# A hybrid decoder layer on one core: keeping split weights in DRAM, and a triangular inverse spread over 128 partitions

## The chip, the cores and the metric

The kernel runs on one core of one Trainium2 chip. The metric is the device time of one execution in microseconds, taken as the median of several runs.

## The reference

One decoder layer works on 2,048 tokens of width 1,024, in float32. It has two mixers side by side and a feed-forward part behind them:

```python
h = _rmsnorm(x, norm1_w[l])
proj = h @ w_in[l]                      # 1024 x 3840 columns, for HGRN2 and RWKV-7
q_raw, f_raw, i_raw, g_raw = ...        # HGRN2: 4 heads of 128, chunkwise gated recurrence
o_hg = _hgrn2_mixer(...)                # S_t = diag(f_t) S_{t-1} + k_t v_t^T ; o_t = S_t^T q_t
rw_p = rw_p + (_token_shift(rw_p) - rw_p) * rw_shift_mu[l]
o_rw = _rwkv7_mixer(...)                # S_t = S_{t-1} diag(w_t) + (S_{t-1} a_t) b_t^T + v_t k_t^T
x = x + concat([o_hg, o_rw]) @ w_out[l]
x = x + _conv_ffn(_rmsnorm(x, norm2_w[l]), w_up[l], conv_w[l], conv_b[l], w_down[l])
return _rmsnorm(x, final_norm_w)
```

RWKV-7 has 8 heads of 64. Its recurrence is solved chunk by chunk; for each chunk of 64 tokens a unit triangular matrix is inverted.

## The kernel before

The tokens are cut into four blocks of 512. The first part, `phase1`, does the input projection, both mixers and three of the four output projections; the second part does the last output projection, the FFN and the closing norm. Only `phase1` is edited.

Every large matmul is made of three. A float32 operand is split into a high part `h` (a cast on ScalarE, line 243) and a low part `l` (a subtraction on VectorE, line 244), and `mm3` adds h·h, h·l and l·h (lines 259 to 261).

Three generators run side by side in `phase1`, and a loop takes one step of each of two of them in turn and then fills about 2 us with the third:

- `dense` is the stream of projections. Each block has 30 columns of 128 output features. For a column, `load` (line 546) brings the weights from `w_in` in two halves of 256 KB into `wraw`, a ring of four buffers, and splits each into `wh` and `wl`, rings of four buffers each; so two columns fit, and the raw ring runs ahead of them. A column is 24 large matmuls. The same 30 columns come again in every block, and are loaded and split again. Between the columns stand the output projections of earlier blocks (`out_block`, which loads `woraw`), transposes and norms.
- `rw_super` is RWKV-7, two super-blocks a block, eight in all. It makes the matrices `M` (matmuls of line 695), sends a part of them by DMA through DRAM (`Ed`, lines 711 and 713) into `E`, where 64 partitions hold one 32 x 32 triangle each (two of the four 32 x 32 quarters per chunk are triangles), and inverts them on VectorE in 31 steps of a product (line 764) and a sum (line 766) into `Ti`. Then `Ti` and its transpose `TiT` go to DRAM (`Td`, lines 770 and 772) and come back in another layout, into `TZ` (line 782, 4 transfers) and `TTs` (line 779, 8 transfers). Matmuls `z` (line 790), `z2` (line 803) and `qu` (line 816) put the inverse together and apply it; ScalarE copies the result out of PSUM into `M` and `UV`; `yg` (line 841) and a scan of eight steps (line 875) follow.
- `hg_unit` is HGRN2, four heads a block. Six levels of doubling (`scaled`, lines 934 to 939) scale q and k by products of the gates; each level is four VectorE products of half a block's elements: X for odd and even positions, `Sf` and `Pf`.

All weight loads and nearly all other transfers go through the queue of the sync engine (SP), which issues them in order and stops at the first whose buffer or source is not ready. GpSimd is nearly without work in the kernel before. The order of each engine's instructions is set by a scheduler from the program's order and the dependencies.

Of the kernel before, what the change touches and what calls it, by code (L numbers as in the profile page):

```python
# [18 lines left out]
P = 128  # L19
# [4 lines left out]
NBLK = T // BLK  # L24
# [37 lines left out]
def tile_layer(ctx, tc, consts, x, norm1_w, w_in, hg_lb_logits, hg_norm_w, rw_shift_mu, rw_w0, rw_w2,  # L62
# [46 lines left out]
    def act(out_, in_, func, **kw):  # L109

        want = tables.get(func)
        if want is not None and want != tab["now"]:
            pre = S.preload_act_table_set(want)
            for u_ in tab["uses"]:
                tc.add_manual_dep(pre.ins, u_.ins.name, NOSYNC, reason="table order")
            tab.update(now=want, pre=pre, uses=[])
        i_ = S.activation(out_, in_, func, **kw)
# [121 lines left out]
    def split(pool, src, shape, name, bufs):  # L239

        hi = pool.tile(shape, F32R, tag=name + "h", name=name + "h", bufs=bufs)
        lo = pool.tile(shape, F32R, tag=name + "l", name=name + "l", bufs=bufs)
        S.copy(hi, src)  # L243
        V.tensor_sub(lo, src, hi.bitcast(F32))  # L244
        return hi, lo
# [17 lines left out]
    def phase1(c1):  # L263
        hp = c1.enter_context(tc.tile_pool(name="hp", bufs=1, reuse_waits="tile"))
        wp = c1.enter_context(tc.tile_pool(name="wp", bufs=2, reuse_waits="tile"))
        sp = c1.enter_context(tc.tile_pool(name="sp", bufs=1, reuse_waits="tile"))
        rp = c1.enter_context(tc.tile_pool(name="rp", bufs=1, reuse_waits="tile"))
# [10 lines left out]
        TTs = hp.tile([P, 16, 64], F32, name="TTs")  # L278
# [4 lines left out]
        hl = hp.tile([P, KD, BLK], F32R, name="hl")  # L283
# [214 lines left out]
        def dense():  # L498
# [37 lines left out]
            for i, jb in sorted(extra, key=lambda e: e[0], reverse=True):  # L536
                jobs.insert(i, jb)
            cols = [jb[1] for jb in jobs if jb[0] == "P"]
            loaded = {}

            def load(i):
                if i < len(cols) and i not in loaded:
                    ws = []
                    for k2 in range(2):
                        raw = wp.tile([P, 4, P], F32, tag="wraw", name="wraw", bufs=4)
                        dma(raw, w_in[0, k2 * 512:k2 * 512 + 512, cols[i]:cols[i] + P].rearrange("(k p) c -> p k c", p=P))
                        ws.append(split(wp, raw, [P, 4, P], "w", 4))
                    loaded[i] = ws

            i = 0  # L550
            load(0)
            ahead = iter(())
            for n, jb in enumerate(jobs):
# [26 lines left out]
                ws = loaded.pop(i)  # L580
# [24 lines left out]
        er0 = lambda e: 64 if e == 0 else 0  # L605
# [5 lines left out]
        def col0(u, e):  # L611

            return er0(e) if u == 0 else 64 - er0(e)
# [3 lines left out]
        U = range(2)  # L617

        def rw_super(nb, s_):

            tl = stage[("tl", nb)]
            r, k, v = (stage.pop(("rkv", nb, s_, w)) for w in range(3))
# [10 lines left out]
            a, iW = ai[:, 0], ai[:, 1]  # L633
# [9 lines left out]
            c, km, sq = mk_[:, 0], mk_[:, 1], mk_[:, 2]  # L643
# [70 lines left out]

            KBT = tile_("KBT", [2, 8, P], "KBT")
            for u in U:
# [7 lines left out]
            UV = tile_("UV", [8, 2, P], "UV")  # L724
# [18 lines left out]
            for b, h, e, u in quads():  # L743
                kr, c0, sl = 64 - er0(e), col0(u, e), (b * 2 + h) * 64
# [5 lines left out]
            for e in range(2):  # L750
                r0, c0 = er0(e), col0(1, e)
                act(RHS[r0:r0 + 64, 4:8, :, 64:128], lvv[c0:c0 + 64, 1], AF.Copy)
            yield

            n = 64
            Ti = rp.tile([P, 32, 32], F32, tag="Ti", name="Ti")
            V.memset(Ti[0:n], 0.0)
            V.memset(Ti[0:n].rearrange("m a b -> m (a b)")[:, 0:1024:33], 1.0)
            yield
            for j in range(31):  # L760
                nr, ncol = 31 - j, j + 1
                tmp = rp.tile([P, 272], F32, tag="etmp", name="etmp")
                tv = tmp[0:n, 0:nr * ncol].rearrange("m (a b) -> m a b", b=ncol)
                V.tensor_mul(tv, E[0:n, j, j + 1:32].unsqueeze(2).broadcast_to([n, nr, ncol]),
                             Ti[0:n, j, 0:ncol].unsqueeze(1).broadcast_to([n, nr, ncol]))
# [4 lines left out]
            dma(Td[0], Ti[0:n])  # L770
            V.tensor_copy(TiT[0:n], Ti[0:n].rearrange("m a b -> m b a"))
            dma(Td[1], TiT[0:n])
            TZ = tile_("XH", [2, 2, 4, 2, 32], "TZ")
            for u in U:
                for e in range(2):
                    r0 = er0(e)
                    for q in range(2):
                        m0 = u * 32 + (e * 2 + q) * 8
                        dma(TTs[r0 + 32 * q:r0 + 32 * q + 32, 8 * u:8 * u + 8, 32 * q:32 * q + 32],
                            Td[1, m0:m0 + 8].rearrange("m s t -> s m t"))  # L780
                    m0 = u * 32 + e * 16
                    dma(TZ[r0:r0 + 32, 0, u].rearrange("p b h t -> p (b h) t"),
                        Td[0, m0:m0 + 8].rearrange("m s t -> s m t"))
            for _ in range(2):
                yield
            z = bank2()
            for b, h, e, u in quads():
                r0 = er0(e)
                c0, sl = r0 + 32 - 32 * u, u * 256 + (b * 2 + h) * 32
                TE.matmul(z[c0:c0 + 32, 0, sl:sl + 32], M[r0:r0 + 32, u, e, b, h, 32:64],  # L790
                          TZ[r0:r0 + 32, 0, u, b, h, :], start=True, stop=True, tile_position=(r0, c0))
            for u in U:
                for e in range(2):
                    r1 = er0(e) + 32
                    c0 = r1 - 32 * u
                    act(TZ[r1:r1 + 32, 1, u].rearrange("p b h t -> p (b h t)"),
                        z[c0:c0 + 32, 0, u * 256:u * 256 + 256], AF.Copy)
            yield
            z2 = bank2()
            for b, h, e, u in quads():  # L800
                r0 = er0(e)
# [4 lines left out]
            for u in U:  # L806
                for e in range(2):
                    r0 = er0(e)
# [5 lines left out]
            for b, h, e, u in quads():  # L814
                r0, c0, sl = er0(e), col0(u, e), ((b % 2) * 2 + h) * P
                TE.matmul(qus[u][c0:c0 + 64, b // 2, sl:sl + P], TTs[r0:r0 + 64, u * 8 + b * 2 + h, :],
                          RHS[r0:r0 + 64, 4 * u + b, h, :], start=True, stop=True, tile_position=(r0, c0))
            for u in U:
                quv = qus[u].rearrange("p j (b h t) -> p (j b) h t", h=2, t=P)
                bs = slice(4 * u, 4 * u + 4)  # L820
                if u == 0:
                    act(M[:, u, 0, :, :, 0:64], quv[:, :, :, 0:64], AF.Copy)
                for e in range(2):
                    r0, c0 = er0(e), col0(u, e)
                    if u == 1:
                        act(M[r0:r0 + 64, u, 0, :, :, 0:64], quv[c0:c0 + 64, :, :, 0:64], AF.Copy)
                    act(UV[r0:r0 + 64, bs, e, :].rearrange("p b (h t) -> p b h t", t=64),
                        quv[c0:c0 + 64, :, :, 64:128], AF.Copy)
# [84 lines left out]
        def hg_unit(nb, j):  # L913
# [13 lines left out]
            V.memset(Sf, 1.0)  # L927

            def scaled(l):

                m = 1 << l
                X = rp.tile([P, BLK], F32, tag="hX", name="hX", bufs=3)
                vw = lambda t_: t_.rearrange("p (n e m) -> p n e m", e=2, m=m)
                V.tensor_mul(vw(X)[:, :, 1, :], vw(q)[:, :, 1, :], vw(Pf)[:, :, 1, :])
                V.tensor_mul(vw(X)[:, :, 0, :], vw(k)[:, :, 0, :], vw(Sf)[:, :, 0, :])
                n_ = BLK // (2 * m)
                V.tensor_mul(vw(Sf)[:, :, 0, :], vw(Sf)[:, :, 0, :],
                             vw(Pf)[:, :, 1, m - 1:m].broadcast_to([P, n_, m]))
# [557 lines left out]
```

## Time and profile before

| | |
|---|---|
| median of 3 runs | 2762.55 us (2758.13 to 2766.44) |
| profiled execution | 2766.94 us, span 2765.2 us |
| mean granted TensorE clock | 0.983 |
| instructions | 47,846 |
| HBM read, written | 325.94 MB, 105.91 MB |

The page gives each engine's busy time in the span. The view by stretch gives the same for a window, with the granted clock of TensorE and the share of the DMA engines' time. The view of waits tells which engine's instruction waited for which other instruction: us in total, times, longest. A group of instructions has a line of kernel.py, an engine, an operation, the tiles and the shape, a count, busy us and mean ns, and the idle time before them with what ended it. In the timeline a row is a start, a duration and what ran; SPq is the sync engine's queue of DMA issues.

### The profile page before, as it was taken

What the parts mean: (1) busy time and instruction counts of PE and PEld (TensorE: products, weight loads), DVE (VectorE), ACT (ScalarE), POOL (GpSimd) and SP (SyncE); (2) the same over time, 40 slices, a digit from 0 to 9 for tenths busy, and PEclk for the clock granted to TensorE, in tenths of its full rate; (3) what the DMA queues carried; (4) which work ended last, traced back from release to release, by engine and by line L of the source; (5) the groups of instructions that cost most, each with busy time, mean ns of one, the idle gap of its engine ahead of it and who ended that gap; (6) DMA issues with size and microseconds to landing.
All of it is one profiled execution on the core that took longest, in us unless ns stands there. A gap on an engine that the chain in (4) does not pass through costs nothing. (4 is left out here: it accounts for less than half of the span.)

```text
span 2765.2 us, 47846 instructions
## 1 busy us (share of the span) xinstructions
PE 2650.8 (96%) x18059; PEld 2107.8 (76%) x18059; DVE 2067.1 (75%) x3877; ACT 1426.2 (52%) x2304; POOL 11.1 (0%) x24
## 2 busy tenths in 40 slices
PE   8999999989999999999889999998999999999998
PEld 6877777766776777767667888786888888877887
DVE  5868787685686766768658889988997877677656
ACT  5455354644645446445346755455545555445444
POOL 0000000000000000000000000000000000000000
PEclk9999999989999899999999999999999999999999
DMA  5222322236331443633475358747662223999865
GB/s 164 77 71 67 102 77 72 69 114 188 115 112 55 111 155 123 193 105 90 144 264 170 115 191 265 230 152 228 211 227 92 88 73 132 333 331 317 287 195 185
DMA packets 429629, 435.01 MB, mean 157 GB/s; under 512 B 68704, under 2 KB 288214, under 8 KB 429398
## 3 DMA queue, kind: packets, MB, share of 16 engines
q1 hardware_dynamic: 428337, 429.30, 48.9%
q8 instruction: 142, 2.33, 0.3%
q0 software_dynamic: 992, 2.64, 0.2%
q14 instruction: 90, 0.73, 0.1%
q10 hardware_dynamic: 68, 0.02, 0.0%
HBM read 325.94 MB, written 105.91 MB: 156 GB/s over the span
## 5 line engine op out<-in xcount | busy, mean ns | idle before, releaser
L259 PE MATMUL pj<-hh,wh 128*128 128x512 f32 x960 | 401.5, 418 | 1.3 <-DVE xh L398 1.2
L260 PE MATMUL pj<-hl,wh 128*128 128x512 f32 x960 | 380.7, 397 | 0.0
L261 PE MATMUL pj<-hh,wl 128*128 128x512 f32 x960 | 379.6, 395 | 0.1
L243 ACT CAST wh<-wraw 128x512 fp32r<-128x512 f32 x240 | 147.5, 618 | 312.7 <-PE pj L260 245.4
L259 PE MATMUL ua<-Bh,uwh 128*128 128x512 f32 x704 | 279.0, 396 | 18.5 <-ACT uwh L243 14.0
L261 PE MATMUL ua<-Bh,uwl 128*128 128x512 f32 x704 | 276.4, 393 | 0.5 <-DVE uwl L244 0.5
L260 PE MATMUL ua<-Bl,uwh 128*128 128x512 f32 x704 | 276.5, 393 | 0.0
L244 DVE TENSOR_TENSOR wl<-wraw,wh 128x512 fp32r<-128x512 f32 x240 | 163.8, 686 | 119.1 <-ACT wh L243 116.3
L259 PEld LDWEIGHTS pj<-hh,wh 128*128 128x128 f32 x960 | 181.0, 189 | 53.5 <-issue 11.1
L260 PEld LDWEIGHTS pj<-hl,wh 128*128 128x128 f32 x960 | 181.2, 189 | 41.8 <-issue 7.5
L261 PEld LDWEIGHTS pj<-hh,wl 128*128 128x128 f32 x960 | 180.9, 188 | 40.0 <-DVE wl L244 1.0
L243 ACT CAST uwh<-uraw 128x512 fp32r<-128x512 f32 x220 | 134.1, 617 | 141.6 <-PE ua L260 67.6
L243 ACT CAST dah<-draw 128x512 fp32r<-128x512 f32 x151 | 93.8, 621 | 177.6 <-DMA draw<-Sg 51.2
L244 DVE TENSOR_TENSOR uwl<-uraw,uwh 128x512 fp32r<-128x512 f32 x220 | 147.0, 686 | 49.2 <-ACT uwh L243 49.0
L244 DVE TENSOR_TENSOR dal<-draw,dah 128x512 fp32r<-128x512 f32 x151 | 104.2, 690 | 100.2 <-ACT dah L243 97.7
L259 PEld LDWEIGHTS ua<-Bh,uwh 128*128 128x128 f32 x704 | 133.4, 190 | 48.8 <-ACT uwh L243 14.5
L261 PEld LDWEIGHTS ua<-Bh,uwl 128*128 128x128 f32 x704 | 133.7, 190 | 30.2 <-DVE uwl L244 2.2
L260 PEld LDWEIGHTS ua<-Bl,uwh 128*128 128x128 f32 x704 | 133.6, 190 | 27.1
L259 PE MATMUL ud<-Bh,uwh 128*128 128x512 f32 x352 | 138.0, 392 | 2.0 <-DVE cv L1347 2.0
L261 PE MATMUL ud<-Bh,uwl 128*128 128x512 f32 x352 | 137.1, 389 | 0.0
L260 PE MATMUL ud<-Bl,uwh 128*128 128x512 f32 x352 | 137.0, 389 | 0.0
L260 PE MATMUL da<-dbl,dah 128*128 128x512 f32 x340 | 133.6, 393 | 1.6 <-DVE dbl L244 1.3
(314 smaller groups left out, 5909.6 us busy)
## 6 DMA issues: line engine op xcount, KB each, us to landing
wraw<-in_w_in_dram SPq DMA_DIRECT2D x240, 256.0 KB, 3.3
uraw<-in_w_up_dram SPq DMA_DIRECT2D x176, 256.0 KB, 3.2
woraw<-in_w_out_dram SPq DMA_DIRECT2D x96, 256.0 KB, 3.1
draw<-Sg SPq DMA_DIRECT2D x88, 256.0 KB, 3.0
draw<-Tw SPq DMA_DIRECT2D x88, 256.0 KB, 4.1
gd<-y SPq DMA_DIRECT2D x86, 256.0 KB, 3.1
xt<-x1d SPq DMA_DIRECT2D x32, 512.0 KB, 6.3
draw<-gd SPq DMA_DIRECT2D x63, 256.0 KB, 4.6
```

The costliest lines, as they stand in the source:

```text
L243: S.copy(hi, src)
L244: V.tensor_sub(lo, src, hi.bitcast(F32))
L259: TE.matmul(acc, lh, rh, start=first, stop=False, skip_group_check=skip)
L260: TE.matmul(acc, lh, rl, start=False, stop=False, skip_group_check=skip)
L261: TE.matmul(acc, ll, rh, start=False, stop=last, skip_group_check=skip)
```

## The change

1. Block 0 loads and splits its 30 columns as before, and also stores each `wh` and `wl` to DRAM tiles `Win` (four transfers of 256 KB a column, issued by GpSimd). Blocks 1 to 3 load `wh` and `wl` from there, four transfers a column by SP straight into the split rings, with no cast and no subtraction.
2. The inverse uses 128 partitions. `E` is loaded twice, into both halves; partition 64f + m holds the columns of parity f of triangle m, 16 instead of 32, so step j works on j // 2 + 1 columns instead of j + 1. `TiT` is copied on ScalarE instead of VectorE. `TZ` and `TTs` are fetched once for each parity, 24 transfers instead of 12.
3. In HGRN2's level 0 the factor `Sf` is still 1, so two VectorE products become ScalarE copies.
4. `Ti` and `Sf` are filled by GpSimd instead of VectorE.
5. The ScalarE copies behind `qu` are put in another order: all three into `M` first, then the four into `UV`.

```diff
+            NCOL = len(cols) // NBLK
+            Win = [[[dp.tile([P, 4, P], F32, name=f"Win{ct}{k2}{c}") for c in "hl"] for k2 in range(2)]
+                   for ct in range(NCOL)]
...
             def load(i):
                 if i < len(cols) and i not in loaded:
-                    ws = []
+                    ws, ct = [], cols[i] // P
                     for k2 in range(2):
-                        raw = wp.tile([P, 4, P], F32, tag="wraw", name="wraw", bufs=4)
-                        dma(raw, w_in[0, k2 * 512:k2 * 512 + 512, cols[i]:cols[i] + P].rearrange("(k p) c -> p k c", p=P))
-                        ws.append(split(wp, raw, [P, 4, P], "w", 4))
+                        if i < NCOL:
+                            raw = wp.tile([P, 4, P], F32, tag="wraw", name="wraw", bufs=4)
+                            dma(raw, w_in[0, k2 * 512:k2 * 512 + 512, cols[i]:cols[i] + P].rearrange("(k p) c -> p k c", p=P))
+                            ws.append(split(wp, raw, [P, 4, P], "w", 4))
+                            for c in range(2):
+                                nc.gpsimd.dma_start(Win[ct][k2][c], ws[k2][c].bitcast(F32))
+                        else:
+                            ws.append(tuple(wp.tile([P, 4, P], F32R, tag="w" + c, name="w" + c, bufs=4) for c in "hl"))
+                            for c in range(2):
+                                dma(ws[k2][c].bitcast(F32), Win[ct][k2][c])
...
-            Td = dp.tile([2, 64, 32, 32], F32, tag="Td", name="Td", bufs=2)
+            Td = dp.tile([2, 2, 64, 512], F32, tag="Td", name="Td", bufs=2)
...
-            dma(E[0:64], Ed)
+            for f in range(2):
+                dma(E[64 * f:64 * f + 64], Ed)
...
-            n = 64
-            Ti = rp.tile([P, 32, 32], F32, tag="Ti", name="Ti")
-            V.memset(Ti[0:n], 0.0)
-            V.memset(Ti[0:n].rearrange("m a b -> m (a b)")[:, 0:1024:33], 1.0)
+            Ti = rp.tile([P, 32, 16], F32, tag="Ti", name="Ti")
+            nc.gpsimd.memset(Ti, 0.0)
+            for f in range(2):
+                nc.gpsimd.memset(Ti[64 * f:64 * f + 64].rearrange("m a b -> m (a b)")[:, 16 * f:16 * f + 496:33], 1.0)
             yield
             for j in range(31):
-                nr, ncol = 31 - j, j + 1
+                nr, ncol = 31 - j, j // 2 + 1
...
-                V.tensor_mul(tv, E[0:n, j, j + 1:32].unsqueeze(2).broadcast_to([n, nr, ncol]),
-                             Ti[0:n, j, 0:ncol].unsqueeze(1).broadcast_to([n, nr, ncol]))
-                V.tensor_add(Ti[0:n, j + 1:32, 0:ncol], Ti[0:n, j + 1:32, 0:ncol], tv)
+                V.tensor_mul(tv, E[:, j, j + 1:32].unsqueeze(2).broadcast_to([P, nr, ncol]),
+                             Ti[:, j, 0:ncol].unsqueeze(1).broadcast_to([P, nr, ncol]))
+                V.tensor_add(Ti[:, j + 1:32, 0:ncol], Ti[:, j + 1:32, 0:ncol], tv)
...
-            TiT = rp.tile([P, 32, 32], F32, tag="E", name="TiT")
-            dma(Td[0], Ti[0:n])
-            V.tensor_copy(TiT[0:n], Ti[0:n].rearrange("m a b -> m b a"))
-            dma(Td[1], TiT[0:n])
+            TiT = rp.tile([P, 16, 32], F32, tag="E", name="TiT")
+            dma(Td[0].rearrange("f m n -> (f m) n"), Ti.rearrange("m a b -> m (a b)"))
+            act(TiT, Ti.rearrange("m a b -> m b a"), AF.Copy)
+            dma(Td[1].rearrange("f m n -> (f m) n"), TiT.rearrange("m a b -> m (a b)"))
...
-                        dma(TTs[r0 + 32 * q:r0 + 32 * q + 32, 8 * u:8 * u + 8, 32 * q:32 * q + 32],
-                            Td[1, m0:m0 + 8].rearrange("m s t -> s m t"))
+                        for f in range(2):
+                            dma(TTs[r0 + 32 * q + f:r0 + 32 * q + 32:2, 8 * u:8 * u + 8, 32 * q:32 * q + 32],
+                                Td[1, f, m0:m0 + 8].rearrange("m (c t) -> c m t", t=32))
...
-                    dma(TZ[r0:r0 + 32, 0, u].rearrange("p b h t -> p (b h) t"),
-                        Td[0, m0:m0 + 8].rearrange("m s t -> s m t"))
+                    for f in range(2):
+                        dma(TZ[r0:r0 + 32, 0, u].rearrange("p b h t -> p (b h) t")[:, :, 16 * f:16 * f + 16],
+                            Td[0, f, m0:m0 + 8].rearrange("m (t c) -> t m c", c=16))
...
+            quv = [qus[u].rearrange("p j (b h t) -> p (j b) h t", h=2, t=P) for u in U]
+            act(M[:, 0, 0, :, :, 0:64], quv[0][:, :, :, 0:64], AF.Copy)
+            for e in range(2):
+                r0, c0 = er0(e), col0(1, e)
+                act(M[r0:r0 + 64, 1, 0, :, :, 0:64], quv[1][c0:c0 + 64, :, :, 0:64], AF.Copy)
             for u in U:
...
-            V.memset(Sf, 1.0)
+            nc.gpsimd.memset(Sf, 1.0)
...
-                V.tensor_mul(vw(X)[:, :, 0, :], vw(k)[:, :, 0, :], vw(Sf)[:, :, 0, :])
...
+                if l == 0:
+                    act(vw(X)[:, :, 0, :], vw(k)[:, :, 0, :], AF.Copy)
+                    act(vw(Sf)[:, :, 0, :], vw(Pf)[:, :, 1, :], AF.Copy)
+                else:
+                    V.tensor_mul(vw(X)[:, :, 0, :], vw(k)[:, :, 0, :], vw(Sf)[:, :, 0, :])
...
```

More of the change, by code (lines that the diff above doesn't have):

```diff
@@ L753, in rw_super @@
             yield
[L755 to L758 removed]
+            Ti = rp.tile([P, 32, 16], F32, tag="Ti", name="Ti")
+            nc.gpsimd.memset(Ti, 0.0)
+            for f in range(2):
+                nc.gpsimd.memset(Ti[64 * f:64 * f + 64].rearrange("m a b -> m (a b)")[:, 16 * f:16 * f + 496:33], 1.0)
             yield
             for j in range(31):
[L761 to L766 removed]
+                nr, ncol = 31 - j, j // 2 + 1
+                tmp = rp.tile([P, 144], F32, tag="etmp", name="etmp")
+                tv = tmp[:, 0:nr * ncol].rearrange("m (a b) -> m a b", b=ncol)
+                V.tensor_mul(tv, E[:, j, j + 1:32].unsqueeze(2).broadcast_to([P, nr, ncol]),
+                             Ti[:, j, 0:ncol].unsqueeze(1).broadcast_to([P, nr, ncol]))
+                V.tensor_add(Ti[:, j + 1:32, 0:ncol], Ti[:, j + 1:32, 0:ncol], tv)
                 if j % 4 == 3:
                     yield
[L769 to L772 removed]
+            TiT = rp.tile([P, 16, 32], F32, tag="E", name="TiT")
+            dma(Td[0].rearrange("f m n -> (f m) n"), Ti.rearrange("m a b -> m (a b)"))
+            act(TiT, Ti.rearrange("m a b -> m b a"), AF.Copy)
+            dma(Td[1].rearrange("f m n -> (f m) n"), TiT.rearrange("m a b -> m (a b)"))
             TZ = tile_("XH", [2, 2, 4, 2, 32], "TZ")
@@ L795, in rw_super @@
                     c0 = r1 - 32 * u
-                    act(TZ[r1:r1 + 32, 1, u].rearrange("p b h t -> p (b h t)"),
-                        z[c0:c0 + 32, 0, u * 256:u * 256 + 256], AF.Copy)
+                    act(TZ[r1:r1 + 32, 1, u].rearrange("p b h (c f) -> p (b h) f c", f=2),
+                        z[c0:c0 + 32, 0, u * 256:u * 256 + 256].rearrange("p (s f c) -> p s f c", f=2, c=16), AF.Copy)
             yield
@@ L817, in rw_super @@
                           RHS[r0:r0 + 64, 4 * u + b, h, :], start=True, stop=True, tile_position=(r0, c0))
+            quv = [qus[u].rearrange("p j (b h t) -> p (j b) h t", h=2, t=P) for u in U]
[3 more added lines that the diff above has]
+                act(M[r0:r0 + 64, 1, 0, :, :, 0:64], quv[1][c0:c0 + 64, :, :, 0:64], AF.Copy)
             for u in U:
[L819 to L822, printed above, removed]
                 for e in range(2):
                     r0, c0 = er0(e), col0(u, e)
[L825 to L828, printed above, removed]
+                    act(UV[r0:r0 + 64, 4 * u:4 * u + 4, e, :].rearrange("p b (h t) -> p b h t", t=64),
+                        quv[u][c0:c0 + 64, :, :, 64:128], AF.Copy)
             yield
```

4 lines of the change are left out of this document (2 added, 2 removed).

## The prediction

> **What bounds the kernel now.** I read the page's parts 1 and 2 first, then busy time by stretch, then who PE waited for, and last the queue of the sync engine around one inverse.
>
> ```profile
> span 2765.2 us, 47846 instructions
> PE 2650.8 (96%) x18059; PEld 2107.8 (76%) x18059; DVE 2067.1 (75%) x3877; ACT 1426.2 (52%) x2304; POOL 11.1 (0%) x24
> ```
> ```profile
> 20.00:1320.00 1300.00, 1246.25 (x11385) 965.36 (x11385) 953.64 (x2157) 666.17 (x1077) 2.41 (x4) 0.98 0.37 107
> 580.00:620.00 40.00, 29.95 (x449) 22.86 (x451) 28.02 (x72) 17.05 (x35) 0.00 (x0) 0.79 0.47 136
> 680.00:700.00 20.00, 20.00 (x90) 16.55 (x89) 8.07 (x18) 7.56 (x13) 0.00 (x0) 1.00 0.78 247
> 940.00:980.00 40.00, 33.59 (x470) 25.75 (x471) 29.14 (x69) 17.76 (x34) 0.00 (x0) 0.79 0.54 159
> 1160.00:1200.00 40.00, 36.37 (x353) 26.86 (x353) 29.89 (x79) 13.42 (x26) 0.58 (x1) 0.91 0.58 170
> 1320.00:1380.00 60.00, 52.74 (x739) 40.31 (x736) 34.87 (x84) 22.56 (x45) 0.54 (x1) 0.89 0.45 135
> 1380.00:1500.00 120.00, 106.55 (x494) 85.05 (x493) 79.37 (x129) 66.43 (x109) 0.72 (x1) 0.93 0.68 226
> ```
>
> PE is the bound, 96% of the span. Every edit lies in the first 1,380 us (the mixers); the FFN behind it is untouched. Columns after the stretch's length: PE, PEld, DVE, ACT, POOL busy, then granted clock, DMA share, GB/s. In 20:1320 PE idles only 1300 - 1246.25 = 53.8 us. The idle clusters where a recurrence's inverse ends (580:620, 940:980, 1160:1200, 1320:1380), and there the granted clock falls too. So the change can earn no more than idle and lost clock. PE's work itself is not edited: 9,192 large (512-column) matmuls in both instruction orders. Who PE waited for between 20 and 1320 us:
>
> ```profile
> PE rw L841 <- ACT UV L117: 8.7, 9, 2.1
> PE hg L997 <- DVE hk L990: 6.4, 5, 2.0
> PE pj L259 <- ACT wh L243: 6.2, 8, 1.6
> PE rw L695 <- DVE KB L683: 4.4, 6, 1.1
> PE hg L955 <- DVE hk L916: 4.1, 2, 2.9
> PE pj L260 <- DVE wl L244: 3.3, 5, 1.9
> PE hg L955 <- DVE hX L934: 2.4, 4, 1.2
> PE rw L790 <- DMA TZ<-Td: 1.7, 2, 1.2
> ```
>
> Most is DVE arriving late, which is what a lighter DVE helps. These five DVE rows hold 6.4 + 4.4 + 4.1 + 3.3 + 2.4 = 20.6 us.
>
> **The change part by part.** *Weights.* Blocks 1 to 3 no longer split 2 x 30 weight halves each, 180 casts and 180 subtractions:
>
> ```profile
> L244 DVE TENSOR_TENSOR wl<-wraw,wh 128x512 fp32r<-128x512 f32 x240 | 163.8, 686 | 119.1 <-ACT wh L243 116.3 <-ACT mk L117 1.0 <-PE pj L260 0.9
> L243 ACT CAST wh<-wraw 128x512 fp32r<-128x512 f32 x240 | 147.5, 618 | 312.7 <-PE pj L260 245.4 <-issue 35.8 <-DMA wraw<-in_w_in_dram 23.4
> ```
>
> DVE loses 180 x 0.686 = 123 us, ACT 180 x 0.618 = 111 us, and ACT no longer stands in line for PE before a cast (245 us of idle ended by PE). All that lies beside PE work, so its direct worth is zero; it pays through the waits above.
>
> *Inverse.* 62 operations per recurrence, on 128 partitions with half the columns each:
>
> ```profile
> 564.79 0.41 DVE L764 TENSOR_TENSOR etmp<-E,Ti 64x256 f32<-64x256 f32 x1
> ...
> 587.92 0.18 DVE L764 TENSOR_TENSOR etmp<-E,Ti 64x31 f32<-64x31 f32 x1
> ```
>
> 225 elements cost 0.23 us, 1.02 ns each. The sum of (31-j)(j+1) is 5,456 elements, that of (31-j)(j//2+1) is 2,856: 2 x 2,600 x 1.02 ns = 5.3 us less per recurrence, 42 us in eight. This is on the chain E, inverse, Td, TZ, z.
>
> *Fills and first level.* The fills leave DVE for GpSimd, and 32 level-0 products become ACT copies:
>
> ```profile
> L927 DVE MEMSET Sf<- x16: 485/485/485, 1.2 to 1309.9; 128x512 f32 x16
> 16.15 0.52 POOL L277 MEMSET Sc<- 128x512 f32 x1
> L935 DVE TENSOR_TENSOR hX<-hk,Sf 128x256 f32<-128x256 f32 x112 | 46.8, 418 | 0.1
> L117 ACT ACTIVATE Af<-A 64x256 f32<-64x256 f32 x32 | 13.3, 414 | 35.6 <-DVE A L961 35.3
> ```
>
> DVE loses 16 x 0.485 + 32 x 0.418 = 21 us, ACT gains about 32 x 0.41 = 13 us, having lost 111; GpSimd is idle. Worth zero alone.
>
> *What is added to the sync queue.* Per recurrence the transfers TZ and TTs double from 12 to 24. One batch (first super-block of block 1):
>
> ```profile
> 435.68 0.51 SPq L770 DMA_DIRECT2D Td<-Ti  x1
> ...
> 438.97 0.87 SPq L782 DMA_DIRECT2D TZ<-Td  x2
> 440.82 2.77 SPq L779 DMA_DIRECT2D TTs<-Td  x6
> ...
> 445.12 0.45 SPq L782 DMA_DIRECT2D TZ<-Td  x1
> ```
> ```profile
> woraw<-in_w_out_dram SPq DMA_DIRECT2D x96, 256.0 KB, 3.1
> TZ<-Td SPq DMA_DIRECT2D x32, 32.0 KB, 1.8
> ```
>
> The batch takes 445.57 - 438.97 = 6.6 us; twelve more issues at about 0.46 us add 5.5 (near half its measured length) to 6.6; I take 6.2. The last TZ lands at 445.1 + 1.8 = 446.9. Who needs it:
>
> ```profile
> 450.69 0.25 PE L790 MATMUL rw<-TZ,M 32*32 32x32 f32 x4
> ...
> 453.36 0.70 PE L790 MATMUL rw<-TZ,M 32*32 32x32 f32 x58
> ```
> ```profile
> 959.32 1.06 PE L790 MATMUL rw<-TZ,M 32*32 32x32 f32 x58 [1.18 <-DMA TZ<-Td]
> ```
>
> In block 1 the bulk of z starts at 453.4, 6.5 us after that landing: this slack swallows the 6.2. In the second super-block of block 2 there is none (1.18 us waited). Against it the inverse ends earlier: by its own 5.3 us, plus splits no longer in DVE's line. Between the last M matmul and the first z matmul of block 1's first super-block PE has 176 large matmuls, 7.3 columns of 24, hence 15 subtractions, 10 us. Less 6.2 for the batch and 0.5 for the second E load, the chain is about 8.6 us shorter. Where an out-projection fills the time (about 4 columns, 8 subtractions, 5.5 us) it is 5.3 + 5.5 - 6.7 = 4 us shorter. The changed instruction order assumes as much: there z's bulk stands 51 large matmuls earlier (1191 to 1140; 11.3 us at 0.222 us each, the pace of 680:700, 20 us for 90). Order gains 11.3, chain 8.6: slack falls from 6.5 to about 3.8, not below zero.
>
> A page's rule speaks against these pieces. The Trainium skill, DMA: Bandwidth & Descriptors (Specifications), puts full line rate at 512 B or more and says smaller transfers read-modify-write; TZ now moves 64 B pieces. By it each TZ might take twice its 1.8 us and the last land 1.8 us later, which only a place without slack would feel: 2744 instead of 2742. The 128 B pieces of now land in 1.8, less than woraw's 3.1 with 2 KB, so the trace shows issue, not bytes, as the price.
>
> *Weight loads behind the batch.* A loaded split pair waits on SP for PE to leave its buffer, where the old raw loads had four extra buffers ahead. Buffers hold two columns: from release (half of column i-1) to use (column i+1) PE has 36 large matmuls, 36 x 0.222 = 8 us plus what is interleaved; a load lands in 3.1 to 3.3. In 680:700 the out-projection already feeds PE at 247 GB/s with PE 20.00 of 20.00, so the plain stream fits. Behind Td, its landing (438.97 - 435.68 = 3.3) and 24 issues (6.6 + 6.2) the queue is shut for 16 us after the inverse's end, and the next weight half lands 3.2 later, at 19.3. By the order its use falls right behind z's bulk; that stands 453.36 - 435.68 = 17.7 after the inverse now, 11.3 earlier by the order, while the inverse ends 5.3 + 10 - 0.5 = 14.8 earlier: 21.2. Close: 0 to 6.2 us each in six recurrences, 0 to 37; I take 1 each, 6.
>
> *Stores of block 0.* 120 on GpSimd:
>
> ```profile
> L1029 POOL DMA_DIRECT2D oT<-osq x4: 542/552/580, 1165.1 to 1364.1; - x4
> ```
>
> 120 x 0.55 = 66 us over a quarter of 1,320: hidden, while a store is done within the two columns that its buffer lives. *Copies of M ahead of UV* release the first of two PSUM pairs two copies later, 0 to 1.2 us in each of eight (estimate from the UV row's waits, at most 2.1); more matmuls now stand ahead (12 for 9), so I take 2 in all.
>
> **Sum.** (a) Waits on DVE: half of 20.6, 10 (0 to 20.6). (b) Clock: busy times (1 - clock) in the four clusters, 29.95 x 0.21 + 33.59 x 0.21 + 36.37 x 0.09 + 52.74 x 0.11 = 22.4; if half the idle goes, 11 (0 to 22.4). (c) Tail: idle 7.3 + 13.5 in 1320:1500, last chain about 8 shorter, part of it covered by other waits: 7 (0 to 20.8). (d) Queue: +6 (0 to 37). (e) Order of copies: +2 (0 to 9.6). Net -20. The profiled execution took 2766.94 (its span and 1.7 around it): 2747. The median of the runs, 2762.55, lies 4.4 lower: **2742 us**.
>
> **Rivals.** *The queue decides (slower).* If real z and weights come when the batch ends, six recurrences lose 6.2 each, 37 us, and the clock with it: in 580:620, 10 idle us cost 6.3 in clock, so 37 cost about 20 more. Less 27 of the gains: +30, 2792. For: SP is one line, the split buffers hold two columns where raw and split held four, and 959.32 shows no slack. Against: the 6.5 us of slack. It decides once the queue is shut for 2 us longer than I count (21.2 against 19.3). Chance 0.27.
> *No change.* DVE's savings lie beside a PE that is 96% busy; idle just moves to ACT rows (UV, wh of the out-projection stays): 2762. Against: four of five big waits are DVE's. 0.08.
> *All idle and clock return:* 20.6 + 22.4 + 20.8 less 8 = 56: 2707. 0.07.
> *Stores held up.* If GpSimd's descriptors wait for a DVE operation, a store takes 0.55 plus up to 0.5 (a fill's length); if one in four then holds a split buffer, 30 x 0.5 = 15 us: 2757. The Trainium skill, SBUF — State Buffer (SBUF: two separate sides), describes just that: GpSimd cannot write descriptors while DVE runs a two-port operation. The few stores of the trace (0.54 to 0.58) do not show it. 0.03.
> That the edits are not carried out is excluded by the instruction order: 360 loads and 120 stores stand in it.
>
> **How the numbers follow.** 0.3% is 8.3 us, about what can be told from no change. The forecast's case has 0.55, of it 0.47 faster and 0.08 within; the queue 0.27, slower but for 0.01; no change 0.06 within, 0.01 either side; full return 0.07 faster; stores 0.03 within. Faster 0.55, same 0.18, slower 0.27. The range takes in the full return and the queue's case: 2705 to 2797; the forecast's own is 2718 to 2762.
>
> **What would show it.** Right: PE idle in 20:1320 falls from 53.8 to about 40, the clock in the clusters rises, z's bulk waits under 1 us for TZ, the rows hk and KB halve, DVE busy falls by some 190 us. Wrong: PE rows that wait for DMA wh, wl or TZ with over 20 us, granted clock under 0.98 in blocks 1 to 3, or ACT idle ended by a store in block 0.

## The result and the profile after

The changed kernel takes 2798.89 us (median of 4 runs, 2796.75 to 2803.4) against 2763.45 for the kernel before on the same chip: a ratio of 1.0129, 95% interval 1.0115 to 1.0143. It is slower by 1.3%, where 2742 us was forecast; 2798.89 lies just above the upper end of the range, and 6.9 us above the rival *the queue decides* (2792).

The top of the page of the kernel after, and its stretches (length, then busy us of PE, PEld, DVE, ACT and POOL, granted clock, DMA share, GB/s):

```profile
span 2795.0 us, 48126 instructions
PE 2657.7 (95%) x18059; PEld 2114.3 (76%) x18059; DVE 1895.8 (68%) x3625; ACT 1352.7 (48%) x2164; POOL 90.2 (3%) x184
```
```profile
20.00:1320.00 1300.00, 1225.66 (x11192) 950.25 (x11191) 763.17 (x1839) 578.32 (x914) 76.50 (x153) 0.96 0.53 166
...
1380.00:2720.00 1340.00, 1305.10 (x5911) 1061.69 (x5902) 1038.06 (x1580) 700.59 (x1104) 2.35 (x4) 0.99 0.62 205
```
```profile
300.00:320.00 20.00, 12.54 (x168) 7.96 (x170) 4.98 (x14) 4.21 (x10) 0.00 (x0) 0.65 0.60 181
448.00:464.00 16.00, 10.37 (x115) 7.33 (x117) 5.34 (x11) 5.71 (x18) 0.00 (x0) 0.86 0.39 96
```

VectorE is busy for 171 us less (2067.1 to 1895.8), near the 190 that were counted, and PE's idle time in 20:1320 did not fall from 53.8 us but rose to 1300 - 1225.66 = 74.3, with a granted clock of 0.96 for 0.98. PE's first up-projection matmul of the FFN (`ua`), where the unedited part begins, starts at 1488.7 us for 1456.2 before, and from 1380 us on PE is about as busy as before (1306.46 us in the same stretch), so the loss is all ahead of the FFN. It lies in new holes behind an inverse, such as 300:320 and 448:464: PE busy 12.54 of 20 and 10.37 of 16. Whom PE waited for there, by the view of waits from 20 to 1320 us of the kernel after (us in total, times, longest):

```profile
PE rw L803 <- DMA TZ<-Td: 37.7, 10, 8.3
PE pj L259 <- ACT wh L243: 7.6, 9, 1.7
...
PE hg L1013 <- DVE hk L1006: 2.0, 3, 1.5
PE rw L853 <- ACT UV L117: 1.7, 3, 1.4
PE hg L971 <- DVE hX L946: 1.5, 2, 0.8
...
PE pj L259 <- DMA wh<-Win190h: 1.0, 1, 1.0
PE pj L260 <- DVE wl L244: 0.9, 3, 0.4
...
PE rw L705 <- DVE KB L693: 0.8, 2, 0.5
PE hg L971 <- DVE hk L928: 0.8, 2, 0.4
```

The rows that a lighter VectorE was to shorten did shorten: the two hk rows from 6.4 + 4.1 to 2.0 + 0.8, KB from 4.4 to 0.8, wl from 3.3 to 0.9. In their place stands one row that had 1.7 us before: z waits 37.7 us for TZ. The sync engine's queue and PE around the third inverse, whose last step starts at 441.9:

```profile
442.16 0.32 SPq L781 DMA_DIRECT2D Td<-Ti  x1
443.24 0.32 SPq L783 DMA_DIRECT2D Td<-TiT  x1
444.17 0.81 SPq L795 DMA_DIRECT2D TZ<-Td  x2
445.28 5.10 SPq L791 DMA_DIRECT2D TTs<-Td  x8
450.43 1.08 SPq L795 DMA_DIRECT2D TZ<-Td  x2
451.55 2.50 SPq L791 DMA_DIRECT2D TTs<-Td  x4
454.09 1.08 SPq L795 DMA_DIRECT2D TZ<-Td  x2
455.22 2.49 SPq L791 DMA_DIRECT2D TTs<-Td  x4
457.75 1.10 SPq L795 DMA_DIRECT2D TZ<-Td  x2
458.95 0.40 SPq L557 DMA_DIRECT2D wh<-Win191h  x1
```
```profile
456.63 0.34 PE L803 MATMUL rw<-TZ,M 32*32 32x32 f32 x4 [1.98 <-DMA TZ<-Td]
460.42 1.03 PE L803 MATMUL rw<-TZ,M 32*32 32x32 f32 x58 [3.45 <-DMA TZ<-Td]
```

The batch lasts from 444.17 to 458.85, 14.7 us for 6.6 before. Its last TZ goes out at about 458.4, and z's bulk starts 2.0 us later, after a wait of 3.45 behind one of 1.98. Most of the 14.7 us are TTs issues, and one of them has become longer than it was. The rows of the tile view, of the kernel before and of the one after (ns min/median/max):

```profile
L779 SPq DMA_DIRECT2D TTs<-Td x64: 302/449/1369, 143.8 to 1330.9; - x64
```
```profile
L791 SPq DMA_DIRECT2D TTs<-Td x128: 555/598/1787, 141.9 to 1355.0; - x128
L795 SPq DMA_DIRECT2D TZ<-Td x64: 318/452/602, 140.4 to 1356.3; - x64
```

### The profile page after: what moved, and what is told of

The parts are those of the page before. It is cut to its first block, busy times and chain, and to the rows that moved or that the text cites. A ratio compares the mean times of both kernels' runs of the same rounds, so it can differ in the third digit from the quotient of the medians.

```text
span 2795.0 us, 48126 instructions
## 1 busy us (share of the span) xinstructions
PE 2657.7 (95%) x18059; PEld 2114.3 (76%) x18059; DVE 1895.8 (68%) x3625; ACT 1352.7 (48%) x2164; POOL 90.2 (3%) x184
## 4 chain that ended last, share of the span: by engine, by line
PE 73%; DVE 8%; DMA 8%; ACT 4%; SPq 3%; issue 3%; DVEq 0%; ACTq 0%
PE pj L259 8%; PE pj L260 7%; PE pj L261 7%; PE ua L259 6%; PE ua L260 6%; PE ua L261 5%; PE ud L259 3%; PE ud L260 3%; PE ud L261 3%; SPq L791 2%; PE da L260 2%; PE da L259 2%; PE da L261 2%; PE hg L971 2%; PE db L261 1%
## 5 line engine op out<-in xcount | busy, mean ns | idle before, releaser
L261 PEld LDWEIGHTS pj<-hh,wl 128*128 128x128 f32 x960 | 181.6, 189 | 39.5 <-issue 0.2
L261 PE MATMUL da<-dbh,dal 128*128 128x512 f32 x340 | 133.0, 391 | 0.0
L259 PE MATMUL da<-dbh,dah 128*128 128x512 f32 x340 | 128.7, 393 | 3.0 <-ACT dbh L243 3.0
```

What stands on the lines that cost most here:

```text
L259: TE.matmul(acc, lh, rh, start=first, stop=False, skip_group_check=skip)
L261: TE.matmul(acc, ll, rh, start=False, stop=last, skip_group_check=skip)
```

## The experiments

Theory: the doubled fetch batch on the sync engine's queue delays z, and that costs the time. Rivals: the kept weights behind the batch; the 128-partition inverse or its double E load itself; the order of the instructions.

All ratios are against the kernel before on the same chip, with 95% intervals. The columns in us are means over the eight recurrences, read from starts in each timeline: *inverse* runs from the start of the first to the start of the last of its operations, and its end here is that last start. PE idle is 1300 less its busy time in 20:1320.

| kernel | inverse | its end to issue of the last TZ | PE idle | median | ratio |
|---|---|---|---|---|---|
| before | 40.6 | 10.4 | 53.8 | 2763.45 | 1 |
| after | 29.9 | 17.9 | 74.3 | 2798.89 | 1.0129 (1.0115 to 1.0143) |
| inv64 | 36.9 | 9.9 | 50.5 | 2765.40 | 1.0016 (1.0005 to 1.0028) |
| inv128_only | 34.4 | 18.1 | 57.0 | 2772.82 | 1.0035 (1.0024 to 1.0047) |
| b_double | 40.7 | 16.3 | 68.0 | 2794.99 | 1.0105 (1.0088 to 1.0121) |
| contig | 30.3 | 14.4 | 56.2 | 2776.02 | 1.0053 (1.0038 to 1.0068) |
| store_int | 30.1 | 11.7 | 55.0 | 2764.30 | 1.0014 (1.0004 to 1.0024) |
| tz_first | 29.7 | 6.6 (TTs at 17.4) | 61.8 | 2773.68 | 1.0037 (1.0023 to 1.0052) |
| before_pool | 40.8 | 6.1 | 50.9 | 2755.55 | 0.9965 (0.9948 to 0.9982) |
| tts_pool | 29.9 | 6.9 | 43.8 | 2735.41 | 0.9900 (0.9882 to 0.9918) |
| pool_nokeep | 33.9 | 7.2 | 52.7 | 2747.23 | 0.9934 (0.9918 to 0.9950) |
| pool_oldcopies | 30.0 | 6.8 | 45.4 | 2732.40 | 0.9880 (0.9863 to 0.9898) |
| pool_e2 | 30.3 | 6.9 | 43.8 | 2734.13 | 0.9907 (0.9884 to 0.9931) |
| best | 30.1 | 7.2 | 45.8 | 2742.66 | 0.9926 (0.9910 to 0.9943) |

**inv64: the change without its inverse.**

```diff
-            for f in range(2):
-                dma(E[64 * f:64 * f + 64], Ed)
+            dma(E[0:64], Ed)
...
-            Ti = rp.tile([P, 32, 16], F32, tag="Ti", name="Ti")
+            Ti = rp.tile([P, 32, 32], F32, tag="Ti", name="Ti")
...
-                nr, ncol = 31 - j, j // 2 + 1
+                nr, ncol = 31 - j, j + 1
...
```

> The changed kernel with the inverse back on 64 partitions and 12 fetches of TZ and TTs, everything else of the change kept. Theory Q (the 24 fetches keep PE waiting for TZ, 38 us in the profile after, and the clock falls with it): waits of z for TZ under 5 us, time 2745 to 2768, near or below the kernel before. Rival W (the loads and stores of the kept weights are what costs): 2785 or more, TZ waits gone and waits for wh or a lower clock in their place.

Measured: 1.0016. The kept weights, the fills, the first level and the copies' order are not what costs the 1.3%. Nor do they bring anything by themselves. PE's waits of inv64, from 20 to 1320 us:

```profile
PE rw L800 <- DMA TZ<-Td: 8.4, 5, 3.3
PE pj L259 <- ACT wh L243: 7.0, 7, 1.5
PE rw L866 <- DVE AR L856: 5.6, 5, 1.8
PE hg L1010 <- DVE hk L1003: 4.0, 4, 2.7
```

Some VectorE rows are shorter here too (this hk row was 6.4), and TZ has 8.4 us for 1.7 before (under 5 were expected), with a batch no longer than before: of what the lighter VectorE freed, PE spent part waiting for z.

**inv128_only: the inverse alone.** The kernel before, with the 128-partition inverse and its 24 fetches.

```diff
-                nr, ncol = 31 - j, j + 1
+                nr, ncol = 31 - j, j // 2 + 1
...
+                        for f in range(2):
+                            dma(TTs[r0 + 32 * q + f:r0 + 32 * q + 32:2, 8 * u:8 * u + 8, 32 * q:32 * q + 32],
...
```

> The kernel before with the inverse on 128 partitions alone (two E loads, 24 fetches), weights split in every block, fills on VectorE. Theory Q: PE waits for TZ by 20 to 45 us, 2780 to 2805. Rival W: the inverse is harmless or helps, 2750 to 2765.

Measured: 1.0035, below what was expected, and PE waits 11.0 us for TZ, not 37.7. So the two halves of the change cost 0.16% and 0.35% apart, and 1.29% together. What differs between this kernel and the one after, with the same batch, is where z stands in PE's order. Counted in the traces, its last matmul follows 840, 1200, 1908 and 2640 large input-projection matmuls in the second, third, fifth and seventh recurrence here, and 792, 1140, 1848 and 2592 in the kernel after (827, 1191, 1901 and 2650 before). So with all edits together the order places z some 50 matmuls sooner, and the batch does not follow. That this place is the cause of the difference fits the waits; z was not moved by itself.

**tz_first: the eight TZ issued ahead of the sixteen TTs**, all still on the sync engine's queue.

```diff
+            for u in U:
+                for e in range(2):
+                    r0, m0 = er0(e), u * 32 + e * 16
+                    for f in range(2):
+                        dma(TZ[r0:r0 + 32, 0, u].rearrange("p b h t -> p (b h) t")[:, :, 16 * f:16 * f + 16],
+                            Td[0, f, m0:m0 + 8].rearrange("m (t c) -> t m c", c=16))
             for u in U:
                 for e in range(2):
...
-                    for f in range(2):
-                        dma(TZ[r0:r0 + 32, 0, u].rearrange("p b h t -> p (b h) t")[:, :, 16 * f:16 * f + 16],
-                            Td[0, f, m0:m0 + 8].rearrange("m (t c) -> t m c", c=16))
```

> The changed kernel, with the eight TZ fetches of a recurrence issued ahead of the sixteen TTs fetches; same count. Theory Q says that z waits for the last TZ because TTs stand ahead of it: waits of z for TZ fall from 38 to under 12 us, part of it comes back as waits of z2 (which needs TTs), 2768 to 2790. If instead the number of transfers in flight or their landing is at fault, the order changes nothing, 2795 to 2803.

Measured: 1.0037. The wait moved from z to z2, by PE's waits of this kernel (20 to 1320 us):

```profile
PE rw L818 <- DMA TTs<-Td: 30.3, 11, 5.2
...
PE rw L805 <- DMA TZ<-Td: 1.6, 2, 0.9
```

z comes early and z2 stands right behind it, so a batch of the same length is waited for one step later: 0.9% better than after, not a gain over before.

**tts_pool: TZ first on the sync engine's queue, TTs issued by GpSimd.**

```diff
-                            dma(TTs[r0 + 32 * q + f:r0 + 32 * q + 32:2, 8 * u:8 * u + 8, 32 * q:32 * q + 32],
+                            nc.gpsimd.dma_start(TTs[r0 + 32 * q + f:r0 + 32 * q + 32:2, 8 * u:8 * u + 8, 32 * q:32 * q + 32],
                                 Td[1, f, m0:m0 + 8].rearrange("m (c t) -> c m t", t=32))
...
```

> The changed kernel with the sixteen TTs fetches of a recurrence issued by GpSimd, the eight TZ fetches by SP. Theory Q (serial issue on one queue): the batch on SP falls from 14.7 us to about 4, waits of z for TZ under 8 us, 2745 to 2770. If landing of many small pieces is at fault, waits stay over 25 us and 2790 or more.

Measured: 0.9900, better than expected and 63 us less than after. Of these, 25 us are the order (tz_first against after) and 38 the change of queue (tts_pool against tz_first). PE's waits for TZ and TTs are 1.3 and 3.3 us. The stretch of this kernel:

```profile
20.00:1320.00 1300.00, 1256.19 (x11589) 973.11 (x11590) 794.55 (x1929) 599.98 (x955) 146.44 (x284) 0.98 0.54 171
```

**b_double: the kernel before, each fetch cut in two**, 24 issues of half the bytes, inverse untouched.

```diff
-                        dma(TTs[r0 + 32 * q:r0 + 32 * q + 32, 8 * u:8 * u + 8, 32 * q:32 * q + 32],
-                            Td[1, m0:m0 + 8].rearrange("m s t -> s m t"))
+                        for f in range(2):
+                            p0 = r0 + 32 * q + 16 * f
+                            dma(TTs[p0:p0 + 16, 8 * u:8 * u + 8, 32 * q:32 * q + 32],
+                                Td[1, m0:m0 + 8, 16 * f:16 * f + 16].rearrange("m s t -> s m t"))
...
```

> The kernel before with each TTs and TZ fetch cut in two (16 contiguous partitions, half the columns): 24 issues, the same bytes, nothing else. Theory Q, the number of issues: the batch grows from 6.5 us to 12 or more (14.7 if an issue for 16 partitions is dear in itself, about 12 if the stride of two partitions made it so), PE waits for TZ 5 to 30 us, 2768 to 2785. If the issues alone cost nothing, 2758 to 2766.

Measured: 1.0105, worse than expected: 29 us for a batch that is 16.3 - 10.4 = 5.9 us longer, 4.9 us of time for each us. Doubling the issues is enough to lose four fifths of what the change loses. It also shows what a TTs issue costs to 16 neighbouring partitions, 429 ns and not 598:

```profile
L781 SPq DMA_DIRECT2D TTs<-Td x128: 303/429/1647, 144.8 to 1367.5; - x128
```

Here the order puts z later (its last matmul follows 840 and 1212 large ones in the second and third recurrence), PE waits only 7.7 us for TZ, and the time is lost all the same (PE idle 68.0). Its longest row is now a VectorE one of HGRN2, `hk`, with 12.5 us for 6.4 before. That a later z puts off all that follows in the recurrence would explain it, but it is not shown.

**contig: the kernel after, TTs written to 16 neighbouring partitions** in place of every second one.

```diff
-                            dma(TTs[r0 + 32 * q + f:r0 + 32 * q + 32:2, 8 * u:8 * u + 8, 32 * q:32 * q + 32],
+                            dma(TTs[r0 + 32 * q + 16 * f:r0 + 32 * q + 16 * f + 16, 8 * u:8 * u + 8, 32 * q:32 * q + 32],
```

> The changed kernel, with each TTs transfer written to 16 neighbouring partitions in place of every second one of 32 (rows of TTs then stand in another order, so the inverse is applied wrongly; counts, bytes and order of the instructions are the same). If the step of two partitions makes a TTs issue 0.60 us: 0.43 to 0.45 us an issue as in the doubled fetches of the kernel before, a batch of about 12.2 us for 14.7, and 2799 - 2.5 x 4.7 = about 2787 us (2780 to 2793). If it is the source, read in the two parities' halves: 0.60 us an issue and 2795 to 2802.

Measured: 1.0053, a median 22.9 us below that of after (21 us by the ratios) and below the 2780 to 2793 that were expected. The tile view of contig, and its waits:

```profile
L791 SPq DMA_DIRECT2D TTs<-Td x128: 302/429/1343, 140.2 to 1331.3; - x128
```
```profile
PE rw L803 <- DMA TZ<-Td: 22.3, 8, 5.1
```

So the step of two partitions in the destination is what makes an issue 0.60 us: 128 x 0.169 = 21.6 us less on the queue, and 21 to 22.9 in the kernel's time. z stands at the same place in both orders (792, 1140, 1848, 2592), so this is the price of the queue alone.

**store_int: the parities interleaved by the stores** of Ti and TiT, so that 12 fetches do again.

```diff
-            dma(Td[0].rearrange("f m n -> (f m) n"), Ti.rearrange("m a b -> m (a b)"))
+            for f in range(2):
+                dma(Td[0].rearrange("m (t f c) -> m f t c", f=2, c=16)[:, f], Ti[64 * f:64 * f + 64])
...
```

> The changed kernel, with the interleaving of the two parities moved from the fetches to the stores: Ti and TiT are stored in two transfers each (one a parity) into the place that a fetch of before reads, so TZ and TTs come back in 12 transfers, as before the change, all on the sync engine's queue. If the length of the batch in front of z is what cost the time: a batch of about 6.5 us again for 14.7, PE's waits for TZ below 5 us for 38, and, with the 4.7 us of span that each us of batch cost in the doubled fetches of the kernel before (+29 us for +6.2), 8.2 x 4.7 = 38 us less than the changed kernel: 2740 to 2765 us. If it is the double load of E, the kept weights on the queue or the 128-partition steps themselves: 2780 to 2800. If the small pieces of the stores (64 bytes) land late: PE's waits for TZ stay near 38 us with a short batch.

Measured: 1.0014, at the upper end of the interval of the batch theory; the kernel after loses 34.6 us by the medians (32 by the ratios) to its 24 fetches, less what the new stores cost. It is no gain over before, though the inverse is 10.5 us shorter. The stores have become dearer: Td<-Ti took 0.32 us in one issue (442.16 above) and now has two of 0.76 in the median, as the tile view says, and TZ is still waited for, 17.6 us where below 5 were expected:

```profile
L782 SPq DMA_DIRECT2D Td<-Ti x16: 550/762/3113, 137.7 to 1310.1; - x16
```
```profile
PE rw L803 <- DMA TZ<-Td: 17.6, 8, 4.3
```

**before_pool: the kernel before, with TZ first and TTs by GpSimd.**

```diff
-                        dma(TTs[r0 + 32 * q:r0 + 32 * q + 32, 8 * u:8 * u + 8, 32 * q:32 * q + 32],
+                        nc.gpsimd.dma_start(TTs[r0 + 32 * q:r0 + 32 * q + 32, 8 * u:8 * u + 8, 32 * q:32 * q + 32],
                             Td[1, m0:m0 + 8].rearrange("m s t -> s m t"))
...
```

> The kernel before with the eight TTs fetches issued by GpSimd, the four TZ by SP. If a shorter stretch of SP is worth something even where PE hardly waits for TZ (1.7 us), 2750 to 2760; if only the wait of z counts, 2758 to 2766.

Measured: 0.9965. Already in the kernel before, where PE waited 1.7 us for TZ, 4.3 us less to the last TZ, with TTs on the other queue, are worth 0.35%, some 9 us.

**pool_nokeep: tts_pool with the weights loaded and split in every block.**

```diff
-                            for c in range(2):
-                                nc.gpsimd.dma_start(Win[ct][k2][c], ws[k2][c].bitcast(F32))
...
```

> The version with TTs on GpSimd (2735), but weights split anew in every block, so without stores and without loads of kept weights. If the kept weights are worth what VectorE and ScalarE lose (234 us beside PE), through the waits on them, 2745 to 2760; if they are worth nothing, as in the run with the inverse on 64 partitions, 2732 to 2740.

Measured: 0.9934 for 0.9900 with the kept weights. Once z is not held up they are worth 12 us by the medians, 9 by the ratios (whose intervals just touch). Its inverse takes 33.9 us for 29.9: the splits in VectorE's line.

**pool_oldcopies: tts_pool with the copies behind qu in the order of before.**

```diff
...
-            act(M[:, 0, 0, :, :, 0:64], quv[0][:, :, :, 0:64], AF.Copy)
-            for e in range(2):
-                r0, c0 = er0(e), col0(1, e)
-                act(M[r0:r0 + 64, 1, 0, :, :, 0:64], quv[1][c0:c0 + 64, :, :, 0:64], AF.Copy)
...
+                if u == 0:
+                    act(M[:, u, 0, :, :, 0:64], quv[:, :, :, 0:64], AF.Copy)
...
+                    if u == 1:
+                        act(M[r0:r0 + 64, u, 0, :, :, 0:64], quv[c0:c0 + 64, :, :, 0:64], AF.Copy)
```

> The version with TTs on GpSimd (2735), with the copies behind qu in the order of before (M, UV, UV, then M, M, UV, UV). The step (e) of the prediction put the new order at +2 us (0 to 9.6): so 2726 to 2735 and less wait of PE for the sum into AR; if the new order helps, 2737 to 2745.

Measured: 0.9880, 2732.40 us, the fastest kernel of the study: 1.2% faster than before, 66 us faster than after. By the medians the new order of copies costs about 3 us, but the intervals of the two ratios overlap, so a cost is not shown. The third recurrence, by the timeline, on the sync engine's queue, GpSimd and PE; the last step of the inverse starts at 427.8:

```profile
430.07 3.77 SPq L789 DMA_DIRECT2D TZ<-Td  x8
433.94 0.40 SPq L557 DMA_DIRECT2D wh<-Win191h  x1
```
```profile
431.67 9.12 POOL L797 DMA_DIRECT2D TTs<-Td  x16 [0.64 <-DMA Td<-TiT]
```
```profile
436.98 0.70 PE L805 MATMUL rw<-TZ,M 32*32 32x32 f32 x58
```

z's bulk stands 9.2 us behind the inverse's end (18.5 in after), without a wait, and the weights' queue is free 6.1 us behind it, for 17.1.

**best: pool_oldcopies with the stores and the 12 fetches of store_int.**

```diff
-            dma(Td[1].rearrange("f m n -> (f m) n"), TiT.rearrange("m a b -> m (a b)"))
+            for f in range(2):
+                dma(Td[1].rearrange("m (c f t) -> m f c t", f=2, t=32)[:, f], TiT[64 * f:64 * f + 64])
...
-                    for f in range(2):
-                        dma(TZ[r0:r0 + 32, 0, u].rearrange("p b h t -> p (b h) t")[:, :, 16 * f:16 * f + 16],
-                            Td[0, f, m0:m0 + 8].rearrange("m (t c) -> t m c", c=16))
+                    dma(TZ[r0:r0 + 32, 0, u].rearrange("p b h t -> p (b h) t"),
+                        Td[0, m0:m0 + 8].rearrange("m (t x) -> t m x", x=32))
...
```

> The interleaved stores with 12 fetches, the four of TZ first on the sync engine's queue and the eight of TTs issued by GpSimd, and the copies behind qu in the order of before. If the batch is the price: TZ issued in about 1.4 us for 3.4 and TTs by GpSimd in 8 x 0.55 = 4.4 us for 8, so z2 starts some 3 to 4 us sooner in each recurrence than in the fastest kernel so far (2732): 2712 to 2730 us. If z2 waits for z and its copy anyway, or the two more stores give it back: 2728 to 2736.

Measured: 0.9926, against 0.9880 without the edit, slower than either case expected. The dearer stores take back what the fewer TZ fetches save: 7.2 us to the last TZ, against 6.8 in the table, and z2 starts 1.5 us later behind the inverse in the mean (13.8 for 12.3). But its last matmul ends 1.9 us sooner (20.4 for 22.4), so why the kernel is 10 us slower stays open.

**pool_e2: pool_oldcopies, the second load of E issued by GpSimd.**

```diff
-                dma(E[64 * f:64 * f + 64], Ed)
+                (nc.gpsimd.dma_start if f else dma)(E[64 * f:64 * f + 64], Ed)
...
```

> The fastest kernel so far (TZ first on the sync engine's queue, TTs by GpSimd, copies behind qu in the order of before: 2732 us) with the second load of E issued by GpSimd beside the first instead of behind it. In the changed kernel the inverse starts 4.5 to 7 us after the first E issue, in the kernel before mostly 3.3 to 4. If the second issue on one queue is what starts the inverse later: the first step some 0.6 to 2 us sooner in each of the 8 recurrences, and, at about one us of span for each us on this path where nothing covers it, 2 to 8 us less: 2724 to 2730 us. If GpSimd's transfer lands no sooner, or the order puts z earlier by as much: 2730 to 2735 us.

Measured: 0.9907, no gain: the first step comes 5.7 us after the first E issue in the mean of the eight recurrences, and 5.8 in pool_oldcopies (4.6 before). But the two loads did not go out together: in each recurrence the second issue, on whichever queue, starts 0.5 to 1.4 us after the first. So the run does not tell whether the second issue is what delays the first step against the kernel before; that stays open.

## Why the prediction was wrong

**The step that failed is the one on the queue and its slack:** "Order gains 11.3, chain 8.6: slack falls from 6.5 to about 3.8, not below zero." In the recurrence on which it was worked out, the third, the chain from the E issue to the end of the batch went from 53.8 to 51.6 us, 2.2 shorter and not 8.6. It begins at these issues, before and after:

```profile
391.74 0.47 SPq L713 DMA_DIRECT2D E<-Ed  x1
```
```profile
407.26 1.14 SPq L724 DMA_DIRECT2D E<-Ed  x2
```

Its pieces: inverse 39.5 to 29.1 (-10.4) and its end to the first TZ 3.9 to 2.3 (-1.6), together 12.0 for the forecast 15.3; the E load +1.6 for 0.5; the batch 6.6 to 14.7, +8.1 for 6.2. (The 128-partition steps gave what was counted: the inverse falls from 40.6 to 34.4 us in inv128_only, 6.2 for 5.3. The splits gave less: in the mean the inverse falls by another 4.5 us, from inv128_only to after, for the 10 of the forecast.)

The order also gained more than was counted. From the E issue to z's bulk PE took 453.36 - 391.74 = 61.6 us before; after, it took 460.42 - 407.26 = 53.2, and 47.7 without the 1.98 + 3.45 = 5.4 us of waits for TZ. That is 13.9 sooner for the forecast 11.3, which took 51 matmuls at the pace of a stretch that is full of large ones. So the slack is 6.5 - (13.9 - 2.2) = -5.2 us, and 5.4 were waited: sign and size come out. The sum of the prediction had no term for z waiting for TZ at all.

**How much each piece cost.** From 2742 to 2798.89 it is 56.9 us. By the medians, 22.9 of these are the issue time (21 by the ratios, as before took 2763.45 beside after and 2760.75 beside contig): the forecast took 0.46 us for each new issue from transfers to 32 partitions, and a TTs issue with a step of two takes 0.60 (after against contig). Contig is the kernel with about the batch that I counted (11.8 us for 12.8), and it takes 2776, still slower than before. A further 11.7 are that batch itself (contig against store_int), for which I took only the 6 us of the weights. The last 22.3, store_int's 2764.3 against 2742, are gains that did not come: terms (a), (b) and (c), and with them what the dearer stores cost.

**(a) Waits on VectorE, 10:** the five rows fell by more than that, from 20.6 to 2.0 + 0.8 + 0.8 + 0.9 and 1.5 for hX, 6.0. But the time passed to the TZ row, in part in inv64 too, where nothing was added to the batch. That a row of waits falls does not give its time back while the next thing in PE's order is late. **(b), (c) clock and tail:** the granted clock in 20:1320 fell to 0.96. With z's inputs off the queue the sum was about right: idle 43.8 and 2735 us in tts_pool, against "about 40" and 2742.

**(d) The weights behind the batch, 6:** PE's waits for weights kept in DRAM are 1.4 us in all, though the next half is issued 17.1 us after the inverse's end (16 forecast). The half of the rival *the queue decides* that spoke of z was right; the half on weights was not. That the waits add up to 37.7 us for its 37 is luck: it meant 6.2 us in each of six recurrences, and the 37.7 are 4.1 to 11.5 us in five. I gave it 0.27 because of a slack read in one recurrence; in the fourth and the sixth, where z waited for TZ even before (0.5 and 1.2 us), it now waits 11.5 and 9.7. The prediction names the sixth and its missing slack, and still put nothing into the sum for it.

**(e) The order of the copies, 2:** about 3 by the medians (tts_pool against pool_oldcopies), not clear of the noise.

**The stores of block 0:** the 120 stores took 0.54 us in the median and 0.65 at most, and no operation of ScalarE or VectorE in block 0 waits for one. The rule of the Trainium skill, SBUF — State Buffer (SBUF: two separate sides), that a two-port operation of VectorE keeps GpSimd from writing descriptors, did not show in them, nor in the TTs issues of tts_pool (0.53). **Small pieces:** TZ in pieces of 64 bytes landed in 1.9 us for 1.8, so the line-rate rule of the Trainium skill, DMA: Bandwidth & Descriptors (Specifications), changed nothing in the fetches that can be seen. In the stores of store_int it may have: 128 KB of Ti in pieces of 64 bytes landed in 4.5 us in the median, where in the kernel after 256 KB of TiT in pieces of 2 KB landed in 2.4. One that would have helped stands in the Trainium skill, Trainium Kernel Development and Optimization (Key Constraints): issuing from several engines saves only the sequencer's issue time. The runs agree, and here that issue time was worth 38 us, between tz_first and tts_pool.

## What to carry to other kernels

Count a batch of transfers on one queue by the issue time of its own form (partitions, step, number) and put the whole of it on the path of whoever reads the last one; in this kernel each us in front of z, in the mean, cost 4.3 to 6.5 us of time over its eight recurrences (contig against store_int, after against contig). When an edit makes an engine lighter, look up in the new instruction order how much sooner the dependents are placed, and subtract only what their whole chain, transfers included, became shorter. Before splitting a transfer for the sake of an engine, see if an idle engine can issue part of it: the same change with TZ first and TTs issued by GpSimd is 1.0% faster than before instead of 1.3% slower.

## What the runs showed of the hardware

A 16 KB fetch from DRAM to 16 neighbouring partitions takes 0.43 us to issue on the sync engine's queue, as long as a 32 KB one to 32 partitions (0.45), and 0.60 us when the 16 partitions lie two apart; the landing takes 1.7 and 2.1 us. GpSimd issues the form with the step in 0.53 us, and the one to 32 partitions in 0.58, but these land later: in 3.3 us (tts_pool) and 3.9 or 5.5 us (before_pool, best) in the median, for 2.1 and 1.9 from the sync engine's queue. Storing 64 partitions in pieces of 64 bytes takes 0.76 us to issue in the median (up to 3.1), where 128 partitions of 2 KB in a row take 0.32.
